# Latent attention in a hybrid decoder layer: a first set of scores for the maxima, a second set laid out as [key, query]

## The chip, the cores and the metric

The kernel runs on one core of a Trainium2 chip. The metric is the device time of one execution in microseconds (us), as the median of the runs shown. A core has five engines that work side by side and wait for each other by semaphores: TensorE (PE; its weight loads are listed apart as PEld), VectorE (DVE), ScalarE (ACT), GpSimd (POOL) and SyncE (SP), which here only issues DMA transfers. Each engine works through its own instructions in a fixed order, so an instruction that waits holds up everything behind it on that engine.

## The reference

Two decoder layers work on one sequence of 1024 tokens of width 1024, in float32. Each layer multiplies x by `w_in`, runs three token mixers on slices of the result, concatenates them, multiplies by `w_o`, normalizes, and ends with a gated feed-forward part. The mixers are stick-breaking attention (4 heads), multi-head latent attention (MLA, 4 heads) and RWKV-7 (8 heads). The change concerns MLA above all, and one instruction of stick-breaking:

```python
def causal_softmax_attention(q, k, v, scale):        # MLA: q, k have 96 columns per head, v has 64
    s = einsum('bhqd,bhkd->bhqk', qb, k) * scale
    s = where(kpos <= qpos, s, neg)
    p = softmax(s, axis=-1)
    return einsum('bhqk,bhkd->bhqd', p, v)

def stick_breaking_attention(q, k, v):               # 4 heads of 64
    z = einsum('bhqd,bhkd->bhqk', qb, k) * scale
    log_keep = where(past, log_sigmoid(-z), 0)
    log_later = cumsum(log_keep, reverse=True) - log_keep
    w = where(past, exp(log_sigmoid(z) + log_later), 0)
    return einsum('bhqk,bhkd->bhqd', w, v)

mix = concatenate([o_sb, o_mla, o_rwkv], axis=-1) @ w_o
x = layer_norm(DEEPNORM_ALPHA * x + mix, ln1_g, ln1_b)
```

## The kernel before

Matmuls that must be exact to float32 are made of three in the format float32r: each operand is split into a high part and a rest, and `mm3` adds high x high, high x rest and rest x high into one accumulator. The values are plain float32.

A layer runs in stages: `phase_a` (projections, MLA's preparation, RWKV), then the attention stage in `run`, then `oproj` (the product with `w_o` and the first normalization), then `ffn`. Every mixer writes its output into `mixd` in DRAM, as 8 blocks of 128 rows (channels) by 1024 tokens; `mix_load(i)` reads all 8 blocks for the 128 tokens of tile i and splits them, and `oproj` takes the tiles from i = 7 down to 0. `wo_load(l, k)` reads row block k of `w_o`; blocks 2 to 5 go into four buffers named `pst`, and blocks 0, 1, 6 and 7 share the two buffers named `raw` with the tiles that `mix_load` reads.

In the attention stage four generators are drawn from in turn, one query block of 128 tokens at a time: two for MLA (`mla`, hp = 0 and 1, each working through two heads) and two for stick-breaking (`stick`). The list `seq`, built from STREAM_ORDER, sets the turns, and MLA_AHEAD blocks of MLA come ahead of them all. The second head of each generator takes its query blocks in falling order (`range(NT)[:: 1 - 2 * pr]`), so that the block of tokens 7 is written early in the second half. A scheduler of the framework then sets the final order on every engine, from the order of the code and the offsets in PRIORITY.

One MLA block (`mla_block`, `mla_post`) works with queries on the partitions: scores [128 queries, up to 1024 keys] in one or two pieces of at most 512 columns (`sc`, two PSUM banks), causal mask by one more matmul, maximum on DVE, the running negative maximum on DVE, exponential on ACT with its row sum, a correction factor and a reciprocal, and the normalization of the probabilities on DVE:

```python
nc.vector.reduce_max(c(0), s, axis=AX.X)
nc.scalar.activation(e[:, a0:a1], s, AF.Exp, scale=sc, bias=c(2), accum_out=c(4))
nc.vector.tensor_scalar(e[:, a0:a1], e[:, a0:a1], st[:, 6:7], None, op0=ALU.mult)
```

`w_transpose` turns the probabilities into [key, query] with one TensorE transpose per 128x128 block and an ACT copy out of PSUM, `attn_out` multiplies them with V, and `av_store` copies 64 rows of the result and issues the store to `mixd`.

One stick-breaking block (`stick_block`, `stick_post`) has two matmuls per piece, a tanh on ACT, a mask on POOL, then on DVE `kp = 0.5 - 0.5 * be` (line 385), a scan and a product; transposes, values and store go as above, through the PSUM banks `pa`.

Of the kernel before, what the change touches and what calls it, by code (L numbers as in the profile page):

```python
# [9 lines left out]
F32 = mybir.dt.float32  # L10
# [31 lines left out]
MLA_AHEAD = 4  # L42
STREAM_ORDER = (-3, 0, 0, 1)
# [26 lines left out]
class Body:  # L70
# [38 lines left out]
    def constants(self):  # L109
# [40 lines left out]
        nc.vector.memset(self.mhalf, -0.5)  # L150
        self.rmse = self.t(cp, [P, 1], "rmse")
# [229 lines left out]
    def stick_post(self, be, kp, i, LL, nb, n, V, hp, pr, wp):  # L381
# [3 lines left out]
        nc.vector.tensor_scalar(kp[:, : LL - 1], be[:, 1:LL], -0.5, 0.5, op0=ALU.mult, op1=ALU.add)  # L385
# [117 lines left out]
    def mla(self, wp, hp):  # L503
        nc = self.nc
        r96 = slice(0, 96)
        for pr in range(2):
            if hp == 0:
                self.mv = self.t(wp, [P, NT, P], "mv")
                nc.sync.dma_start(self.mv, self.mvd[pr])
            V = self.mv  # L510
            rq, rk = (self.t(self.pp_, [P, S], "pst", bufs=4) for _ in range(2))
            nc.sync.dma_start(rq[r96], self.mqd[2 * pr + hp])
            nc.sync.dma_start(rk[r96], self.mkd[2 * pr + hp])
            qh, ql, kh, kl = (self.t(wp, [P, S], f"{n}{hp}", F32R, bufs=1) for n in ("qh", "ql", "kh", "kl"))
            eng = nc.gpsimd if pr else None
            for h, lo, r in ((kh, kl, rk), (qh, ql, rq)):
                nc.scalar.copy(h[r96], r[r96])
                self.lo4(lo, r, h, r96, SPLIT_MLA[pr])
            for i in range(NT)[:: 1 - 2 * pr]:
                self.mla_block(i, pr, hp, (qh[r96], ql[r96], kh[r96], kl[r96]), V, wp)  # L520
                yield

    def mla_block(self, i, pr, hp, qk, V, wp):
        nc = self.nc
        sc = 96 ** -0.5
        qh, ql, kh, kl = qk
        nb, LL = i + 1, (i + 1) * P
        qs = slice(i * P, i * P + P)
        st = self.t(wp, [P, 12], "mst", bufs=4)
        e = self.t(wp, [P, S], "mexp", bufs=3)  # L530
        pcs = self.pieces(LL)
        n = len(pcs)
        for u, (a0, a1) in enumerate(pcs):
            sp = self.pst("sc")
            s = sp[:, : a1 - a0]
            last = u == n - 1
# [3 lines left out]
            c = lambda o, u=u: st[:, o + u : o + u + 1]  # L540
            nc.vector.reduce_max(c(0), s, axis=AX.X)
            if u:
                nc.vector.tensor_scalar(c(2), c(0), -sc, st[:, 2:3], op0=ALU.mult, op1=ALU.min)
            else:
                nc.vector.tensor_scalar(c(2), c(0), -sc, None, op0=ALU.mult)
# [683 lines left out]
```

## Time and profile before

| | us |
|---|---|
| median of 3 runs (lowest, highest) | 3157.64 (3152.78, 3160.75) |
| the profiled execution's own time | 3154.05 |
| span in its profile | 3152.3 |
| attention stage, layer 0: from the first MLA score to the last attention matmul | about 549 to 747 |
| the same, layer 1 | about 2097 to 2306 |

The span begins with the first instruction and ends with the last. A stage is found by the times of its own instructions; the two attention stages together take 407 us, 13% of the span, and the rest is projections, RWKV and the feed-forward part. In the views an engine is busy while one of its instructions runs; matmuls overlap in the array, so that TensorE can be busy nearly all the time and still not issue at its full rate. The time between the starts of neighbouring matmuls tells what one costs when nothing holds it up.

### The profile page before, as it was taken

The numbers are of one execution on the slowest core, as the hardware profiler recorded it, in microseconds if no ns is written. First come the engines' busy times: TensorE is split into PE (matmuls) and PEld (weight loads), VectorE is DVE, ScalarE is ACT, GpSimd is POOL, SyncE is SP. The second block draws the span as 40 slices with busy tenths as digits, with TensorE's granted clock in tenths as the row PEclk, the third lists the DMA queues.
The fourth block names the chain that finished last, engine by engine and source line by source line (L and its number), as shares of the span: only waits on it lengthen the run. The fifth ranks groups of instructions, "written<-read, shape, count | busy, mean of one in ns | idle before, by whom it ended". The sixth has DMA issues, their size and how long they took to land. (4 is left out here: it accounts for less than half of the span.)

```text
span 3152.3 us, 42021 instructions
## 1 busy us (share of the span) xinstructions
PE 2993.2 (95%) x16572; PEld 2421.2 (77%) x16572; DVE 1796.4 (57%) x2842; ACT 1058.6 (34%) x1865; POOL 330.7 (10%) x346
## 2 busy tenths in 40 slices
PE   8998999988999999999999989999789999999998
PEld 6677777776888888888877767777678888888887
DVE  4587764876644444444746877567865444344436
ACT  5444343764122112222144443446532211122220
POOL 0112131132000000000001111311310000000000
PEclk9999899999999999999999999999899999999999
DMA  4344566323421111111234456662235111111111
GB/s 129 97 141 110 169 186 191 97 62 121 149 85 50 51 41 47 54 50 51 64 84 127 108 132 193 178 190 53 81 121 172 54 47 40 43 56 49 54 47 54
DMA packets 339284, 301.79 MB, mean 96 GB/s; under 512 B 25224, under 2 KB 304016, under 8 KB 339088
## 3 DMA queue, kind: packets, MB, share of 16 engines
q1 hardware_dynamic: 339088, 299.11, 32.1%
q8 instruction: 131, 2.15, 0.3%
q14 instruction: 65, 0.53, 0.1%
HBM read 208.87 MB, written 90.18 MB: 95 GB/s over the span
## 5 line engine op out<-in xcount | busy, mean ns | idle before, releaser
L202 PE MATMUL psmm<-xTh,whi 128*128 128x512 f32 x2144 | 852.9, 398 | 0.0
L204 PE MATMUL psmm<-xTh,wlo 128*128 128x512 f32 x2144 | 852.1, 397 | 0.0
L203 PE MATMUL psmm<-xTl,whi 128*128 128x512 f32 x2144 | 852.1, 397 | 0.0
L197 ACT CAST whi<-raw 128x1024 fp32r<-128x1024 f32 x152 | 159.9, 1052 | 1111.3 <-PE psmm L203 1076.1
L204 PEld LDWEIGHTS psmm<-xTh,wlo 128*128 128x128 f32 x2144 | 405.2, 189 | 93.2 <-issue 4.3
L202 PEld LDWEIGHTS psmm<-xTh,whi 128*128 128x128 f32 x2144 | 405.4, 189 | 92.9 <-issue 4.4
L203 PEld LDWEIGHTS psmm<-xTl,whi 128*128 128x128 f32 x2144 | 405.3, 189 | 92.8 <-issue 3.9
L198 DVE TENSOR_TENSOR wlo<-raw,whi 128x1024 fp32r<-128x1024 f32 x122 | 148.8, 1220 | 424.5 <-ACT whi L197 424.5
L1031 DVE TENSOR_TENSOR y<-y,psps 128x512 f32<-128x512 f32 x288 | 196.2, 686 | 171.8 <-PE psps L204 171.4
L202 PE MATMUL psps<-wdh,hh 128*128 128x512 f32 x672 | 266.8, 397 | 0.0
L203 PE MATMUL psps<-wdl,hh 128*128 128x512 f32 x672 | 263.1, 391 | 0.0
L204 PE MATMUL psps<-wdh,hl 128*128 128x512 f32 x672 | 260.1, 391 | 0.0
L894 POOL TENSOR_TENSOR lrs<-lrs,mhalf 128x1 f32<-128x1 f32 x32 | 29.1, 910 | 1637.7 <-DVE lrs L893 1637.7
L202 PEld LDWEIGHTS psps<-wdh,hh 128*128 128x128 f32 x672 | 126.1, 188 | 36.4 <-ACT hh L197 5.5
L204 PEld LDWEIGHTS psps<-wdh,hl 128*128 128x128 f32 x672 | 126.2, 188 | 27.0
L203 PEld LDWEIGHTS psps<-wdl,hh 128*128 128x128 f32 x672 | 126.3, 188 | 25.8
L1006 DVE TENSOR_TENSOR cv<-cv,psmm 128x1024 f32<-128x1024 f32 x44 | 53.7, 1221 | 143.3 <-PE psmm L204 138.4
L198 DVE TENSOR_TENSOR wdl<-raw,wdh 128x1024 fp32r<-128x1024 f32 x42 | 51.4, 1225 | 88.5 <-ACT wdh L197 88.5
L198 POOL TENSOR_TENSOR wlo<-raw,whi 128x1024 fp32r<-128x1024 f32 x30 | 76.0, 2532 | 242.5 <-ACT whi L197 242.4
L312 PE MATMUL pspa<-Aa,mv 128*128 128x128 f32 x576 | 86.4, 298 | 4.4 <-ACT Aa L328 3.8
L312 PEld LDWEIGHTS pspa<-Aa,mv 128*128 128x128 f32 x576 | 77.1, 207 | 17.5 <-ACT Aa L328 15.8
L820 PE MATMUL pspa<-RBl,PSl 128*128 128x128 f32 x512 | 73.4, 292 | 17.2 <-ACT QC L823 11.8
(443 smaller groups left out, 4777.4 us busy)
## 6 DMA issues: line engine op xcount, KB each, us to landing
raw<-in_ffn_w_up_dram SPq DMA_DIRECT2D x88, 512.0 KB
raw<-in_w_in_dram SPq DMA_DIRECT2D x44, 512.0 KB
raw<-in_ffn_w_down_dram SPq DMA_DIRECT2D x44, 512.0 KB
rbd<-RB SPq DMA_DIRECT2D x64, 256.0 KB
PSl<-psd SPq DMA_DIRECT2D x32, 512.0 KB
RBl<-rbd SPq DMA_DIRECT2D x32, 512.0 KB
psd<-Vz SPq DMA_DIRECT2D x64, 128.0 KB
xxd<-X SPq DMA_DIRECT2D x64, 128.0 KB
```

Of the source, the lines that this page charges most:

```text
L197: self.nc.scalar.copy(hi, src)
L198: (eng or self.nc.vector).tensor_tensor(lo, src, hi.bitcast(F32), op=ALU.subtract)
L202: mm(out, lh, rh, start=start, stop=False)
L203: mm(out, lh, rl, start=False, stop=False)
L204: mm(out, ll, rh, start=False, stop=stop)
L312: self.nc.tensor.matmul(av, V[:, j, :], wt[:, j, :], start=j == 0, stop=j == nb - 1)
L820: nc.tensor.matmul(pQ[:, f, e, :], PSh[:, f, h, e, :], RBh[:, f, h, e, :], start=True, stop=True)
L894: nc.gpsimd.tensor_tensor(rs, rs, self.mhalf[:, 0:1], op=ALU.pow)
L1006: nc.vector.tensor_tensor(cv, cv, pg, op=ALU.mult)
L1031: nc.vector.tensor_tensor(y[:, i, hs], y[:, i, hs], ps, op=ALU.add)
```

## The change

MLA becomes one generator that works through the four heads. For head n it computes all scores as before, but only to take the row maxima (`mla_max`). When all 8 query blocks are done, `mla_row` makes a row of the negative maxima: a reduction over the pieces, a split into a float32r part and its rest, one matmul with the identity that turns columns into rows, a copy on ACT, and two DMA transfers inside SBUF that lay the two parts into rows 96 and 97 of the query operand `qh`. The key operand `kh` holds ones in these rows, and the two rests hold zeros, so the second set of scores (`mla_values`), computed as [key, query] for 512 queries at a time, comes with the maximum already taken off. Its exponential on ACT is the moving operand of the product with V directly. Beside the 64 columns of V stand 64 columns of ones, so that the other half of the accumulator holds the row sums; a reciprocal and a product on DVE finish 512 queries, and one store writes them. The values of head n are drawn from beside the maxima of head n + 1, three units for every two query blocks.

Gone are the running maximum, the row sums from ACT, the correction, the normalization on DVE, the transposes of MLA with their copies, and the order of falling query blocks for MLA. The PSUM banks change from two for `sc` and two for `av` to three and one. In stick-breaking, `kp` is now computed on ACT.

```diff
-MLA_AHEAD = 4
-STREAM_ORDER = (-3, 0, 0, 1)
+MLA_AHEAD = 8
...
-        nc.vector.tensor_scalar(kp[:, : LL - 1], be[:, 1:LL], -0.5, 0.5, op0=ALU.mult, op1=ALU.add)
+        nc.scalar.activation(kp[:, : LL - 1], be[:, 1:LL], AF.Identity, scale=-0.5, bias=self.half)
...
+    def mla_tiles(self, wp):
+        for hp in range(2):
+            ts = {n: self.t(wp, [P, S], f"{n}{hp}", F32R, bufs=1) for n in ("qh", "ql", "kh", "kl")}
+            nc.scalar.copy(ts["kh"][96:98], self.ones[96:98].to_broadcast([2, S]))
+            for n in ("ql", "kl"):
+                nc.scalar.mul(ts[n][96:98], self.ones[96:98].to_broadcast([2, S]), 0.0)
+            V = self.t(wp, [P, NT, P], f"mv{hp}", bufs=1)
+            nc.gpsimd.memset(V[:, :, 64 - 64 * hp : 128 - 64 * hp], 1.0)
...
+    def mla(self, wp):
+        self.mla_tiles(wp)
+        prev = iter(())
+        for n in range(5):
+            if n < 4:
+                pr, hp = n // 2, n % 2
+                ts, V, M = self.mla_load(pr, hp)
...
+                nxt = self.mla_values(wp, pr, hp, ts, V)
+            for i in range(NT):
+                if n < 4:
+                    self.mla_max(i, ts, st)
+                for _ in range(1 + i % 2):
+                    next(prev, None)
+                yield
+            for _ in prev:
+                pass
+            if n < 4:
+                self.mla_row(st, ts, M, wp)
+                prev = nxt
...
+    def mla_row(self, st, ts, M, wp):
+        nc.vector.reduce_max(m, st, axis=AX.X)
+        nc.vector.tensor_scalar(M[:, 0:NT], m, -1.0, None, op0=ALU.mult)
+        nc.vector.scalar_tensor_tensor(M[:, NT : 2 * NT], m, -1.0, M[:, 0:NT].bitcast(F32), op0=ALU.mult, op1=ALU.subtract)
+        nc.tensor.matmul(ps[:, 0:P], M, self.identr, start=True, stop=True)
+        nc.scalar.copy(r[0 : 2 * NT], ps[0 : 2 * NT, 0:P])
+        for u in range(2):
+            nc.sync.dma_start(ts["qh"][96 + u : 97 + u, :].bitcast(F32), r[u * NT : u * NT + NT, :].bitcast(F32))
+
+    def mla_values(self, wp, pr, hp, ts, V):
+        qh, ql, kh, kl = (ts[n][0:98] for n in ("qh", "ql", "kh", "kl"))
...
+        for Q in range(2):
+            q0 = Q * 512
+            av = self.pst("av")
+            nj = 4 * Q + 4
+            for j in range(nj):
+                c0 = max(0, j * P - q0)
...
+                self.mm3(s, kh[:, js], kl[:, js], qh[:, cs], ql[:, cs], True, not dg)
+                if dg:
+                    nc.tensor.matmul(s[:, 0:P], self.negm, self.identr, start=False, stop=True)
+                w = self.t(wp, [P, 512], "mexp", bufs=6)
+                nc.scalar.activation(w[:, c0:512], s, AF.Exp, scale=sc)
+                nc.tensor.matmul(av[:, c0:512], V[:, j, :], w[:, c0:512], start=j == 0, stop=j == nj - 1)
+                if j < nj - 1:
+                    yield
+            nc.vector.reciprocal(rs[hr], av[sr])
+            nc.vector.tensor_tensor(ot[hr], av[hr], rs[hr], op=ALU.mult)
+            nc.sync.dma_start(self.mixd[2 + pr][hr, q0 : q0 + 512], ot[hr])
+            yield
...
-                self.psum(c, sc=(512, 2), av=(512, 2))
+                self.psum(c, sc=(512, 3), av=(512, 1))
...
-                for _, _, g in seq:
-                    next(g, None)
+                for t in range(17):
+                    for g in (ms, st[0], ms, st[1]):
+                        next(g, None)
+                for _ in ms:
+                    pass
```

The program built from each kernel shows the order that the scheduler made of it. First TensorE in the middle of layer 0's attention stage. Before, one query block of an MLA head stands as three score matmuls per piece (`pssc`), the mask (L539), then transposes (L327) and values (L312) of earlier blocks:

```order
L202 MATMUL pssc_5107<-kh_831_4959,qh_829_4957 128x512
L203 MATMUL pssc_5107<-kl_832_4960,qh_829_4957 128x512
L204 MATMUL pssc_5107<-kh_831_4959,ql_830_4958 128x512
L312 MATMUL psav_5049<-Aa_4944,mv_4951 128x128 x4
L202 MATMUL pssc_5114<-kh_831_4959,qh_829_4957 128x256
L203 MATMUL pssc_5114<-kl_832_4960,qh_829_4957 128x256
L204 MATMUL pssc_5114<-kh_831_4959,ql_830_4958 128x256
L539 MATMUL pssc_5114<-negm_67,identr_65 128x128
```

Now a unit of the second set (`psav_5232` takes its exponentials; keys and queries have changed sides) stands beside the first set of the next head:

```order
L203 MATMUL pssc_5327<-qh_827_4953,kh_829_4955 128x512
L204 MATMUL pssc_5327<-ql_828_4954,kh_829_4955 128x512
L205 MATMUL pssc_5327<-qh_827_4953,kl_830_4956 128x512
L602 MATMUL psav_5232<-mexp_5324,mv_831_4960 128x512
L313 MATMUL pspa_5302<-Aa_4946,mv_5098 128x128 x3
L599 MATMUL pssc_5327<-identr_65,negm_67 128x128
L203 MATMUL pssc_5358<-kh_835_4966,qh_833_4964 128x512
L204 MATMUL pssc_5358<-kl_836_4967,qh_833_4964 128x512
L205 MATMUL pssc_5358<-kh_835_4966,ql_834_4965 128x512
```

So the products with V come as single matmuls of up to 512 columns, and no transpose of MLA stands between; the one transposing operation left in the stage is that of stick-breaking.

Second, SP's queue around the end of layer 0's attention stage. Before, the load of the first tile for `oproj` (`raw_7063`, tokens 896 to 1023) and the four blocks of `w_o` that go through `raw` stand among the attention stores (`avo`), with some 15 stores still behind them:

```order
L400 DMA mixd_111<-avo_6537 64x128
L912 DMA raw_7063<-mixd_111 128x8x128
L400 DMA mixd_111<-avo_6572 64x128
L972 DMA raw_7069<-in_w_o_dram 128x1024
L400 DMA mixd_111<-avo_6614 64x128
L972 DMA raw_7071<-in_w_o_dram 128x1024
L400 DMA mixd_111<-avo_6651 64x128
L972 DMA raw_7115<-in_w_o_dram 128x1024
L400 DMA mixd_111<-avo_6684 64x128
L400 DMA mixd_111<-avo_6724 64x128
L972 DMA raw_7119<-in_w_o_dram 128x1024
```

Now they stand behind the last stores of the stage (`mot_6729` is MLA's last 512 tokens), with the normalization's parameters and the residual's tiles among them:

```order
L609 DMA mixd_113<-mot_6729 64x512
L401 DMA mixd_113<-avo_6748 64x128
L958 DMA raw_6751<-mixd_113 128x8x128
L1018 DMA raw_6757<-in_w_o_dram 128x1024
L950 DMA gb_6791<-in_ln_g_dram 128x1024
L950 DMA bb_6793<-in_ln_b_dram 128x1024
L1018 DMA raw_6759<-in_w_o_dram 128x1024
L1018 DMA raw_6803<-in_w_o_dram 128x1024
L984 DMA z_6819<-in_x_dram 128x1024
L984 DMA z_6891<-in_x_dram 128x1024
L1018 DMA raw_6807<-in_w_o_dram 128x1024
L958 DMA raw_6872<-mixd_113 128x8x128
```

All five loads that share the two `raw` buffers, and the next tile's load behind them, have moved past the end of the stage.

Third, TensorE at the same place after the change. `psmm_6821` is tile 7 of `oproj`, `psmm_6893` tile 6:

```order
L602 MATMUL psav_6582<-mexp_6724,mv_837_4971 128x128
L328 MATMUL pspa_6743<-ident_60,mexp_6732 128x128
L313 MATMUL pspa_6746<-Aa_4946,mv_5976 128x128
L203 MATMUL psmm_6821<-w0h_5057,whi_6752 128x512
L204 MATMUL psmm_6821<-w0l_5058,whi_6752 128x512
...
L205 MATMUL psmm_6821<-woh_6789,wlo_6753 128x512
L203 MATMUL psmm_6893<-w0h_5057,whi_6873 128x512
L204 MATMUL psmm_6893<-w0l_5058,whi_6873 128x512
L205 MATMUL psmm_6893<-w0h_5057,wlo_6874 128x512
L203 MATMUL psmm_6893<-w0h_5057,whi_6873 128x512
L204 MATMUL psmm_6893<-w0l_5058,whi_6873 128x512
L203 MATMUL psmm_6821<-w0h_5057,whi_6752 128x512
```

The first product of `oproj` needs tile 7 and block 0 of `w_o`, and the second half of tile 7 stands behind five products that need tile 6; nothing of the attention stage stands beside them.

## Rows read from the trace of the kernel before

**Rows 1.** The page, part 1: busy us, share of the span, instructions of each engine.
```profile
PE 2993.2 (95%) x16572; PEld 2421.2 (77%) x16572; DVE 1796.4 (57%) x2842; ACT 1058.6 (34%) x1865; POOL 330.7 (10%) x346
```

**Rows 2.** Busy by stretch: us, PE, PEld, DVE, ACT, POOL; clock, DMA share, GB/s.
```profile
549.00:747.00 198.00, 173.78 (x1213) 149.15 (x1213) 156.88 (x317) 131.07 (x352) 44.89 (x56) 0.96 0.29 78
2097.00:2306.00 209.00, 176.97 (x1252) 152.36 (x1252) 162.46 (x328) 135.03 (x360) 47.82 (x58) 0.96 0.28 78
590.00:650.00 60.00, 57.38 (x416) 49.59 (x415) 46.02 (x102) 40.21 (x116) 6.14 (x16) 1.00 0.11 27
2305.00:2325.00 20.00, 14.42 (x50) 10.19 (x49) 11.60 (x9) 8.16 (x9) 5.19 (x2) 0.83 0.70 213
```

**Rows 3.** Waits of PE: layer 0's stage (first row), layer 1's (second); total, times, longest.
```profile
PE pspa L327 <- DVE mexp L388: 9.8, 9, 3.1
...
PE pspq L376 <- POOL qh L361: 7.5, 1, 7.5
```

**Rows 4.** Timeline of PE, layer 0: start, us, operation, how many.
```profile
640.45 0.29 PE L202 MATMUL pssc<-kh,qh 96*128 96x256 f32 x1
640.58 0.28 PE L203 MATMUL pssc<-kl,qh 96*128 96x256 f32 x1
641.78 0.93 PE L327 MATMUL psav<-ident,mexp 128*128 128x128 f32 x7
666.49 2.05 PE L312 MATMUL psav<-Aa,mv 128*128 128x128 f32 x16
745.35 0.49 PE L312 MATMUL pspa<-Aa,mv 128*128 128x128 f32 x2
760.09 0.39 PE L202 MATMUL psmm<-woh,whi 128*128 128x512 f32 x1
760.32 0.39 PE L203 MATMUL psmm<-wol,whi 128*128 128x512 f32 x1
763.34 0.39 PE L204 MATMUL psmm<-woh,wlo 128*128 128x512 f32 x1
```

**Rows 5.** Groups of DVE, layer 0's stage: busy us, mean ns, idle before and releaser.
```profile
L541 DVE TENSOR_REDUCE mst<-pssc 128x1 f32<-128x512 f32 (+3 forms) x48 | 26.1, 548 | 7.6 <-PE pssc L204 5.4 <-PE pssc L539 2.1
L561 DVE TENSOR_SCALAR mexp<-mexp,mst 128x256 f32<-128x256 f32 (+3 forms) x32 | 12.3, 388 | 0.2
L559 DVE TENSOR_SCALAR mexp<-mexp,mst 128x512 f32<-128x512 f32 (+1 forms) x16 | 8.6, 535 | 0.5
L385 DVE TENSOR_SCALAR pd<-mexp 128x255 f32<-128x255 f32 (+5 forms) x11 | 5.5, 498 | 3.2 <-POOL mexp L384 3.2
L545 DVE TENSOR_SCALAR mst<-mst 128x1 f32<-128x1 f32 x32 | 4.5, 141 | 0.1
L555 DVE SCALAR_TENSOR_TENSOR mst<-mst 128x1 f32<-128x1 f32 x16 | 4.2, 266 | 11.9 <-ACT mst L554 11.9
L552 DVE RECIPROCAL mst<-mst 128x1 f32<-128x1 f32 x16 | 2.4, 153 | 4.2 <-ACT mexp L546 4.2
```

**Rows 6.** Groups of ACT, the same stretch.
```profile
L328 ACT COPY Aa<-psav 128x512 f32<-128x512 f32 (+3 forms) x48 | 21.7, 479 | 3.7 <-PE psav L327 3.2
L546 ACT ACTIVATION_READ_ACCUMULATOR mexp<-pssc,mst 128x1 f32 x48 | 9.5, 197 | 0.0
L399 ACT ACTIVATE avo<-psav 64x128 f32<-64x128 f32 x32 | 8.7, 270 | 11.1 <-PE psav L312 5.2 <-ACT Aa L328 1.9 <-ACT mst L554 1.5
```

**Rows 7.** Timelines of SP, ACT and DVE, layer 0's handover to `oproj`; last, POOL's group.
```profile
701.13 0.38 SPq L912 DMA_DIRECT2D raw<-mixd  x1
...
755.23 0.38 SPq L912 DMA_DIRECT2D raw<-mixd  x1
...
759.35 1.05 ACT L197 CAST whi<-raw 128x1024 fp32r<-128x1024 f32 x1 [7.40 <-DMA raw<-mixd]
...
760.43 1.23 DVE L198 TENSOR_TENSOR wlo<-raw,whi 128x1024 fp32r<-128x1024 f32 x1 [1.86 <-ACT whi L197]
...
L198 POOL TENSOR_TENSOR w0l<-raw,w0h 128x1024 fp32r<-128x1024 f32 x2 | 6.0, 2978 | 8.1 <-ACT w0h L197 8.1
```

More of the change, by code (lines that the diff above doesn't have):

```diff
@@ L150, in constants @@
         nc.vector.memset(self.mhalf, -0.5)
+        self.half = self.t(cp, [P, 1], "half")
+        nc.vector.memset(self.half, 0.5)
         self.rmse = self.t(cp, [P, 1], "rmse")
@@ L504, in mla, with mla_load @@
+    def mla_load(self, pr, hp):
         nc = self.nc
         r96 = slice(0, 96)
[L506 to L521, printed above, removed]
@@ L523, in mla_block @@
-    def mla_block(self, i, pr, hp, qk, V, wp):
+        ts, V, M = self.mx[hp]
+        rq, rk = (self.t(self.pp_, [P, S], "pst", bufs=4) for _ in range(2))
+        nc.sync.dma_start(rq[r96], self.mqd[2 * pr + hp])
+        nc.sync.dma_start(rk[r96], self.mkd[2 * pr + hp])
+        nc.sync.dma_start(V[:, :, 64 * hp : 64 * hp + 64], self.mvd[pr][:, :, 64 * hp : 64 * hp + 64])
+        for h, lo, r in (("kh", "kl", rk), ("qh", "ql", rq)):
+            nc.scalar.copy(ts[h][r96], r[r96])
+            self.lo4(ts[lo], r, ts[h], r96, SPLIT_MLA[pr])
@@ L524, in mla_block, with mla_max @@
+        return ts, V, M
+    def mla_max(self, i, ts, st):
         nc = self.nc
-        sc = 96 ** -0.5
-        qh, ql, kh, kl = qk
-        nb, LL = i + 1, (i + 1) * P
+        qh, ql, kh, kl = (ts[n][0:96] for n in ("qh", "ql", "kh", "kl"))
+        LL = (i + 1) * P
         qs = slice(i * P, i * P + P)
-        st = self.t(wp, [P, 12], "mst", bufs=4)
-        e = self.t(wp, [P, S], "mexp", bufs=3)
         pcs = self.pieces(LL)
-        n = len(pcs)
         for u, (a0, a1) in enumerate(pcs):
@@ L535, in mla_block @@
             s = sp[:, : a1 - a0]
-            last = u == n - 1
+            last = u == len(pcs) - 1
             self.mm3(s, qh[:, qs], ql[:, qs], kh[:, a0:a1], kl[:, a0:a1], True, not last)
@@ L539, in mla_block @@
                 nc.tensor.matmul(sp[:, a1 - a0 - P : a1 - a0], self.identr, self.negm, start=False, stop=True)
[L540 to L545, printed above, removed]
-            nc.scalar.activation(e[:, a0:a1], s, AF.Exp, scale=sc, bias=c(2), accum_out=c(4))
@@ L547, in mla_block @@
[L547 to L564 removed]
+            nc.vector.reduce_max(st[:, i, u : u + 1], s, axis=AX.X)
@@ L1162, in run @@
             with ExitStack() as c:
-                self.psum(c, sc=(512, 2), av=(512, 2))
+                self.psum(c, sc=(512, 3), av=(512, 1))
                 aw = self.pool(c, "attn", bufs=2, side=side)
-                ms = [self.mla(aw, hp) for hp in range(2)]
+                ms = self.mla(aw)
                 self.wt4 = self.t(self.ip, [P, 6, NT, P], "Aa")
@@ L1170, in run @@
                 for _ in range(MLA_AHEAD):
-                    next(ms[0])
+                    next(ms)
                 cc.close()
@@ L1176, in run @@
                 st = [self.stick(aw3, self.ip, hp) for hp in range(2)]
-                seq = sorted([(t + o, n, g) for n, (g, o) in enumerate(zip((ms[0], st[0], ms[1], st[1]), STREAM_ORDER)) for t in range(17)], key=lambda x: x[:2])
-                for _, _, g in seq:
-                    next(g, None)
+                for t in range(17):
[3 more added lines that the diff above has]
+                    pass
                 nxt = self.mix_load(NT - 1)
```

37 lines of the change are left out of this document (20 added, 17 removed).

## The prediction

> **What bounds the kernel now.** I read the page's first part, then busy time by stretch, then the waits, then timelines. TensorE is busy 2993 of the span's 3152 us [rows 1], so time can be won or lost only where TensorE waits or gets other work. Outside the two attention stages and the steps behind them the edit touches nothing, so the stages are the place: 198 and 209 us, 407 together [rows 2]. There the reader is to see three things: TensorE is busy only 88% and 85% of the time; VectorE is next with 157 of 198 and 162 of 209 us (79% and 78%); ScalarE has 131 of 198. In the best minute of the stage, 590 to 650, TensorE is busy 57.4 of 60 us. What it waits for elsewhere is partly VectorE (9.8 us in layer 0 behind stick-breaking's product, line 388), partly GpSimd (7.5 us in layer 1 behind the split of queries, line 361) [rows 3]. The bound is thus TensorE's own work with a steady loss through its suppliers.
>
> Because overlapped matmuls all count as busy, I count work by spacing instead. At full speed 512 columns cost 0.23 us (760.09 to 760.32), 256 about 0.13 (640.45 to 640.58); 384 lie between, 0.18; a transpose costs (0.93 - 0.27)/6 = 0.11; one record of a 128-column product with V, two of which make a block, (2.05 - 0.27)/15 = 0.119 [rows 4].
>
> **TensorE's work per layer, before.** One head's scores are 12 pieces: five of 512, three of 384, three of 256 and one of 128 columns, 2.17 us, times three matmuls and four heads = 26, plus 32 masks of a block's cost, 3: 29. The transposes are 4 x 36 = 144 at 0.11 = 16; the products 288 at 0.119 = 34. Stick-breaking has two matmuls per piece (17), and the same transposes and products (50): 67. Together 146 to 147. That is 147/198 = 0.74 of layer 0's stage and 147/209 = 0.70 of layer 1's, 0.72 on the whole. In the best minute 416 records at the stage's mean of 147/1213 = 0.121 us make 50.4, or 0.84 of 60 us [rows 2].
>
> **After.** The second scores hold the same 4608 columns a head, with their masks: +29. Gone are MLA's transposes: -16. The products with V move the same columns in fewer records: 0 to -3, taken -2. The four row matmuls are nothing. So 158, 11 more per layer.
>
> **VectorE per layer.** Lines 559, 561, 545, 555 and 552 go: 8.6 + 12.3 + 4.5 + 4.2 + 2.4 = 32; line 385 goes to ScalarE, 32 times about 0.5 = 16 [rows 5]. Line 555's 11.9 us behind ScalarE goes too. The maxima stay (26.1). New are eight products of about 0.65 and four row steps of 0.55: 7. New too are eight reciprocals of 64 x 512 out of PSUM, the change's unknown price. Below, such a tile in one pass costs what line 541's pass does, 0.55 us; above, the one-element reciprocal takes 153 ns against 141 for a plain step of that size, and 12 ns for each element makes 6.3, with the pass about 6.8. One row of one element can't tell a fixed cost from one per element; I take 3.3, half. VectorE then has 157 - 48 + 7 + 26 = 142 (120 to 170 at the ends).
>
> **ScalarE.** MLA's copies (21.7), sum reads (9.5) and output copies (8.7) go [rows 6]; 32 keeps of about 0.6 come (19), four row copies and six fillings of 1024 columns, 1.05 at most each (line 197's cast [rows 7]): 131 falls to about 118. It is no bound before or after, and I price it at nothing; if VectorE were no longer the slower supplier, it would be ScalarE's exponentials that are late next, since the same set of exponentials stays.
>
> **The row's chain.** At each of four head ends the negative maxima pass VectorE, TensorE, ScalarE and two DMAs inside SBUF, before the second scores can start. Stick-breaking and, for three heads, the next head's maxima cover it. A load takes 4.1 us from issue to use [rows 7], so with some 3 for the engines one uncovered end costs about 7; I price none, keeping 14 for the two last ends in the range.
>
> **The stage.** Its time is work over rate. Upwards the rate is bounded by the best minute, 0.84 (188 us a stage, -31 for both); downwards by 0.72 to 0.74 with VectorE no better off (427 for both, +20). I take 0.80, two thirds of the way up: a tenth of VectorE's load and a chain through ScalarE for every block go, but GpSimd's wait and stick-breaking's chain stay. Twice 158/0.80 = 395, -12.
>
> **The handover.** Before, tile 7's load was issued at 701.13, 45 us ahead of the last attention product (745.35 + 0.49 = 745.84, call it T0); tile 7's last product starts at 763.34, T0 + 17.5 [rows 4, 7]. The delay came from blocks of `w_o` that take turns in the two `raw` buffers. In the new order the tile's load and all four blocks stand behind the last stores, which need MLA's last 512 tokens. So: reciprocal and product 4.0, the store's issue 0.4 and its landing about 2.5 (no row shows it; under the 4.1 of a larger load), then the load of tile 7, 4.1 (755.23 to 759.35), and its split, 1.05 on ScalarE and 1.23 on VectorE [rows 7]: T0 + 13. On SP block 0 of `w_o` waits behind that load, lands at T0 + 11.5 and is split at 15.5 (1.05 and GpSimd's 2.98); block 1 follows in the tile's buffer (13 to 20), block 6 in block 0's (15.5 to 23.5), block 7 behind block 1, and tile 6 in block 6's buffer, landing at 27.7 and split at 30. The five products of tile 6 that stand ahead of tile 7's second half hold it until then; 24 products of 0.23 end the tile, T0 + 35.5. That is 18 later; less 1 for the five products already done, and 1 more because ten transfers of 512 KB at the 213 GB/s of layer 1's handover [rows 2] take 24.6 of these 30 us and meet. **+18 per layer, +36 for both.** Ends: +9 (one-pass reciprocal, loads of 3 us that don't meet) and +24 (the slow reciprocal, loads queued behind each other). No work covers it: nothing else is on TensorE's list there. The clock of layer 1's handover is 0.83 against 0.96 in the stage [rows 2], so an idle TensorE also loses some speed afterwards; that is inside the upper end.
>
> **Sum.** Against the profiled execution's 3154 us: -12 + 36 = +24, **3178**. The median of the runs shown, 3157.6, is 3.6 higher, well within the 0.3% (9.5 us) that a measurement of this kernel can tell. This case's own range: rate 0.78 to 0.83 (-2 to -26) and handover +13 to +22 each give 3154 to 3196.
>
> **Rivals.** *Faster: the stage's suppliers were the whole loss.* The rate goes beyond the best minute, to 0.88 (359 us, -48), the reciprocal is one pass, and the handover +13 or 14 each: -21, **3133**. It decides from a rate of about 0.85, where -35 pays the forecast's +36. For it: VectorE's 79% and the waits of [rows 3]; wide products instead of 128-column ones. Against it: no minute of the old stage shows more than 0.84. The Trainium skill, "Perfetto Trace Analysis", section "Identifying the Most-Contended Engine", judges TensorE by weight loads rather than by matmul busy time and would have the engine of highest occupancy improved first. By that rule the stage's bound is VectorE (79% against 149 of 198, 75%, of weight loads), which this change relieves, and the result is this rival; the rows bear it out as far as the two numbers go. Chance 0.20.
>
> *Cancels.* Rate 0.84 to 0.85 and a handover of +16 each: -33 + 32, about **3153**, within 0.3%. Chance 0.15.
>
> *Slower still: the reciprocal.* At 6.8 us, eight of them (54) undo VectorE's relief (170 against 157); each also stops the one bank `av`, so the next unit's product waits behind it, and each layer's last one stands open in the handover. Rate 0.75: 421, +14; handover +19 to 20 with the overlap of loads kept, +38: **3206**. It decides from about 5 us a piece, where VectorE is back at 157. The Trainium skill, "VectorE: DVE Perf Modes", section "First, the fixed hardware budget", says that the reciprocal is an iterative divide with a repeat count of 8. An estimate by that page, eight passes of 512 at one element per 0.96 GHz cycle, would be 4.3 us: VectorE 150, at a rate of 0.79 400 us (-7), the handover +19 each, the sum 3185; no row here shows it. Chance 0.23.
>
> **Numbers.** Forecast 0.42, the rest as above. Nearly all of the forecast's cases and all of the third rival's are slower by over 0.3%: 0.65; within 0.3% 0.15; faster 0.20. The range reaches half into the faster rival at 3136 and past the slow one to 3222, and leaves out about 2 in 10.
>
> **What would show it.** In the profile after: the reciprocal's mean (3 us; 0.6 or 7 are the rivals'); the stage from the first MLA score to the last product, near 197 us; VectorE's busy time there, near 142; the load of tile 7 issued some 7 us after the last product, and tile 7's last product near T0 + 35. A stage under 187 us, or a handover under 25 us, proves the forecast wrong on the fast side; waits of TensorE for the bank `av` or for the row's DMA proves it wrong on the slow one.

## The result, and the profile after

The changed kernel takes 3250.44 us (median of four runs, 3246.35 to 3254.85), the kernel before 3155.89 in the same comparison. The ratio is 1.0298 with a 95% interval of 1.0279 to 1.0318: slower by 3%, some 95 us, where 20 to 24 were forecast. The profiled execution took 3254.85, its span is 3253.1.

The page's first part of the changed kernel (busy us, share of the span, instructions), against [rows 1]:

```profile
PE 3048.8 (94%) x16260; PEld 2429.6 (75%) x16260; DVE 1781.1 (55%) x2547; ACT 1051.2 (32%) x1665; POOL 334.3 (10%) x358
```

VectorE and ScalarE have less to do, as meant, and TensorE 56 us more. Where the time went is seen by stretches. I cut both traces at the same events: a stage from the first MLA score (in layer 1 from RWKV's last product, which comes just before it) to the last product with V; the handover from there to the first transposition of `oproj`'s result.

| profiled execution, us | before | after | difference |
|---|---|---|---|
| stage, layer 0 | 196.6 | 232.3 | +35.7 |
| stage, layer 1 | 202.8 | 231.8 | +29.0 |
| handover, layer 0 | 23.5 | 39.1 | +15.6 |
| handover, layer 1 | 24.4 | 39.4 | +15.0 |
| layer 1's projections and RWKV | 514.1 | 522.5 | +8.4 |
| all else | 2190.9 | 2188.0 | -2.9 |

The handovers came near the forecast (+18 each). The stages, forecast 12 us shorter together, are 65 longer. The 8.4 us in layer 1's RWKV belong to no instruction of the change: the same stretch took between 511 and 522 us in the profiles of the other runs below, and it was long where its mean granted clock was low (0.95 at 522.5 us, 0.97 at 514.1, 0.98 at 511.0), so I count it as variation of single executions.

Busy time by stretch after (length; PE, PEld, DVE, ACT, POOL with their counts; granted clock, DMA share, GB/s): both stages, four pieces of layer 0's, its handover. It answers to [rows 2].

```profile
547.80:780.60 232.80, 192.97 (x1053) 149.19 (x1052) 145.34 (x171) 116.17 (x241) 43.74 (x57) 0.90 0.21 54
2159.50:2391.70 232.20, 192.69 (x1054) 149.31 (x1052) 146.13 (x170) 116.46 (x242) 42.73 (x57) 0.90 0.21 54
...
564.00:572.00 8.00, 2.05 (x7) 1.85 (x8) 3.73 (x8) 3.62 (x5) 0.36 (x2) 0.58 0.57 168
572.00:580.00 8.00, 7.82 (x27) 5.74 (x26) 3.68 (x6) 3.90 (x8) 0.29 (x1) 0.57 0.95 256
580.00:590.00 10.00, 9.18 (x49) 7.00 (x48) 7.51 (x10) 5.83 (x15) 1.17 (x4) 1.00 0.10 23
676.00:684.00 8.00, 3.73 (x11) 2.42 (x11) 5.63 (x4) 2.98 (x5) 7.93 (x7) 0.62 0.42 131
781.00:814.00 33.00, 17.14 (x53) 11.82 (x54) 15.15 (x8) 10.14 (x10) 10.59 (x4) 0.65 0.61 208
```

The two stages before, cut at the same events as here:

```profile
549.00:746.00 197.00, 173.72 (x1213) 149.15 (x1213) 156.88 (x317) 130.10 (x351) 44.89 (x56) 0.96 0.29 78
2102.00:2305.00 203.00, 172.69 (x1220) 149.00 (x1218) 159.20 (x319) 130.73 (x351) 46.08 (x56) 0.96 0.28 76
```

VectorE's 145 us against 142 forecast and ScalarE's 116 against 118: their part of the sum held. TensorE is idle 40 us of each stage where it was idle 23 and 30, and busy 19 and 20 us longer, of which the prediction's count of work explains 11. Its mean clock in the stage is 0.90 where it was 0.96: at two levels, 1.2 and 2.4 GHz, that is about 45 us of layer 0's stage at the lower one, where it was about 17. The other 8 or 9 us of the longer busy time I put down to this clock; that is an estimate from these rows, and no run holds the clock still.

In two of the pieces TensorE does little: it is busy 2.05 us from 564 to 572 and 3.73 from 676 to 684. Behind the first, 572 to 580 is full of matmuls at a clock of 0.57. What it waited for (layer 0's stage; total us, times, longest; [rows 3] before):

```profile
PE pspa L328 <- DVE mexp L389: 17.7, 13, 4.9
PE pspq L377 <- POOL qh L362: 6.2, 1, 6.2
PE pspq L377 <- DVE qh L362: 4.5, 1, 4.5
PE pssc L575 <- DVE mm L573: 2.6, 1, 2.6
```

The last three rows are new in layer 0 at this length (GpSimd's split cost 0.6 us there before). Two are starts of stick-breaking heads (line 377), which now fall on the ends of MLA heads (line 575), so that nothing ahead of them on TensorE's list fills the wait. In layer 1 the wait for GpSimd is not new: it was 7.5 us before [rows 3] and is 6.2 now. The first row is stick-breaking's own chain, 9.8 us before [rows 3]. TensorE's timeline after, at these places and at the end (start, us, operation, idle before and releaser):

```profile
565.40 0.45 PE L575 MATMUL pssc<-identr,mm 128*128 128x128 f32 x1 [2.63 <-DVE mm L573]
...
571.25 0.45 PE L377 MATMUL pspq<-kh,qh 128*128 128x128 f32 x1 [4.55 <-DVE qh L362]
...
572.02 0.63 PE L204 MATMUL pssc<-ql,kh 98*128 98x512 f32 x1
572.45 0.63 PE L205 MATMUL pssc<-qh,kl 98*128 98x512 f32 x1
...
679.04 0.80 PE L377 MATMUL pspq<-kh,qh 128*128 128x512 f32 x1 [6.15 <-POOL qh L362]
...
778.92 0.47 PE L328 MATMUL pspa<-ident,mexp 128*128 128x128 f32 x1 [4.94 <-DVE mexp L389]
779.75 0.80 PE L313 MATMUL pspa<-Aa,mv 128*128 128x128 f32 x2 [0.35 <-ACT Aa L329]
787.94 0.79 PE L203 MATMUL psmm<-w0h,whi 128*128 128x512 f32 x1 [7.39 <-ACT w0h L198]
791.09 0.79 PE L204 MATMUL psmm<-w0l,whi 128*128 128x512 f32 x1 [2.36 <-POOL w0l L199]
...
813.80 0.39 PE L205 MATMUL psmm<-woh,wlo 128*128 128x512 f32 x1
```

After the first hole 512 columns cost 0.43 us (572.02 to 572.45) instead of 0.23: the lower of the two levels, 1.2 GHz. The last product with V ends at 780.55; tile 7's last product of its own starts at 813.80, 33.3 later (35.5 forecast, 17.5 before). VectorE's groups (layer 0's stage), which answer to [rows 5]:

```profile
L606 DVE RECIPROCAL mrs<-psav 64x512 f32<-64x512 f32 x8 | 26.8, 3355 | 9.2 <-PE psav L602 9.1
L566 DVE TENSOR_REDUCE mst<-pssc 128x1 f32<-128x512 f32 (+3 forms) x48 | 25.6, 551 | 36.4 <-PE pssc L205 24.5 <-PE pssc L565 11.6
L388 DVE TENSOR_TENSOR_SCAN LA<-LA,ones 128x255 f32<-128x255 f32 (+4 forms) x10 | 14.2, 1417 | 14.1 <-ACT LA L386 14.1
...
L608 DVE TENSOR_TENSOR mot<-psav,mrs 64x512 f32<-64x512 f32 x8 | 5.5, 687 | 0.2
```

The reciprocal takes 3.36 us (3.3 was taken). VectorE now waits for scores (36.4 us in front of line 566, where the same pass waited 7.6 before [rows 5]). And at the stage's end, VectorE's timeline shows what a long instruction does to those behind it:

```profile
774.02 3.35 DVE L606 RECIPROCAL mrs<-psav 64x512 f32<-64x512 f32 x1 [2.54 <-PE psav L602]
777.40 0.42 DVE L388 TENSOR_TENSOR_SCAN pd<-pd,ones 128x127 f32<-128x127 f32 x1
777.85 0.69 DVE L608 TENSOR_TENSOR mot<-psav,mrs 64x512 f32<-64x512 f32 x1
778.58 0.29 DVE L389 SCALAR_TENSOR_TENSOR mexp<-mexp,pd 128x128 f32<-128x128 f32 x1
```

Stick-breaking's last scan needs 0.42 us and stands behind the reciprocal, and TensorE waits 4.94 for what follows it. SP's timeline closes the chain: MLA's store, stick-breaking's last store, then tile 7's load and `w_o`.

```profile
778.57 0.45 SPq L609 DMA_DIRECT2D mixd<-mot  x1
780.88 0.45 SPq L401 DMA_DIRECT2D mixd<-avo  x1
781.42 0.54 SPq L958 DMA_DIRECT2D raw<-mixd  x1
782.01 0.57 SPq L1018 DMA_DIRECT2D raw<-in_w_o_dram  x1
```

Tile 7's load is issued 0.9 us after the last product, where the prediction looked for 7: MLA's reciprocal, product and store were done before that product ended. Two signs that it gave for the slow side did not come: TensorE waits 0.2 us for the bank `av` in layer 0's stage, and 0.4 us for the row's DMA in layer 1's.

### The profile page after: what moved, and what is told of

Read it like the earlier page. It is cut to its first block, busy times and chain, and to the rows that moved or that the text cites. A ratio compares the mean times of both kernels' runs of the same rounds, so it can differ in the third digit from the quotient of the medians.

```text
span 3253.1 us, 40843 instructions
## 1 busy us (share of the span) xinstructions
PE 3048.8 (94%) x16260; PEld 2429.6 (75%) x16260; DVE 1781.1 (55%) x2547; ACT 1051.2 (32%) x1665; POOL 334.3 (10%) x358
## 4 chain that ended last, share of the span: by engine, by line
PE 74%; DVE 10%; issue 9%; DMA 3%; ACT 2%; POOL 1%; SPq 0%; POOLq 0%; DVEq 0%; ACTq 0%
PE psmm L205 15%; PE psmm L203 15%; PE psmm L204 15%; PE psps L203 5%; PE psps L204 5%; PE psps L205 5%; PE pspa L866 2%; DVE pd L751 1%; PE pspi L810 1%; PE pspa L313 1%; DVE LA L747 1%; PE psmt L214 1%; PE pspa L708 1%; PE psav L602 1%; DMA LA<-xxd 1%
## 5 line engine op out<-in xcount | busy, mean ns | idle before, releaser
L204 PEld LDWEIGHTS psps<-wdl,hh 128*128 128x128 f32 x672 | 126.2, 188 | 25.7
L328 PE MATMUL pspa<-ident,mexp 128*128 128x128 f32 x288 | 61.7, 304 | 34.8 <-DVE mexp L389 34.8
```

The source lines that it names most:

```text
L204: mm(out, lh, rl, start=False, stop=False)
L328: nc.tensor.transpose(pt[:, j * P : j * P + P], w[:, (j0 + j) * P : (j0 + j + 1) * P], self.ident)
```

## The experiments

Times are medians against 3250.4 (changed) or 3155 (before, 3151.6 to 3155.9 from one comparison to the next). The changed kernel was timed in the first comparison only, so a difference of 4 us or less to 3250.4 tells nothing. In the tables "stage" and "handover" are cut as above, layer 0 / layer 1.

**First round: order or suppliers.** The first theories were O, that the stages lost their time by the new order of turns, and S, that the slower supplier (VectorE or ScalarE) still sets the pace.

e1 puts one line back:

```diff
-        nc.scalar.activation(kp[:, : LL - 1], be[:, 1:LL], AF.Identity, scale=-0.5, bias=self.half)
+        nc.vector.tensor_scalar(kp[:, : LL - 1], be[:, 1:LL], -0.5, 0.5, op0=ALU.mult, op1=ALU.add)
```

> The changed kernel with one line of stick-breaking put back: keep is computed on VectorE again. Theory O (order: the 64 us that the two stages lost come from where the new list of turns puts MLA against stick-breaking, so that TensorE has nothing else at the starts of stick-breaking's heads and at the end): within 8 us of the changed kernel's 3250. Theory S (suppliers: ScalarE now stands twice in stick-breaking's chain, and VectorE's 32 us a layer behind ScalarE's keep hold TensorE up): 20 to 40 us faster, 3210 to 3230.

e2 takes out the reciprocal's length:

```diff
-            nc.vector.reciprocal(rs[hr], av[sr])
+            nc.vector.tensor_copy(rs[hr], av[sr])
```

> The changed kernel with MLA's reciprocal replaced by a plain copy of the same 64 x 512 out of PSUM, so the division by the row sums is left out; sixteen reciprocals of 3.36 us become sixteen passes of about 0.7, 21 us of VectorE a layer. Theory O: only the piece at each stage's end and one long stall near 611 us go, 5 to 15 us, 3235 to 3245. Theory S with VectorE as the slower supplier: most of the 42 us of VectorE comes back, 3208 to 3220.

e3 changes one number:

```diff
-MLA_AHEAD = 8
+MLA_AHEAD = 16
```

> The changed kernel with MLA_AHEAD 16 instead of 8: two heads' steps of MLA stand ahead of stick-breaking, MLA's last stores and with them tile 7's load come before stick-breaking's last blocks, and oproj's first products stand beside these. Nothing is computed differently. Theory O: the handover falls by 12 to 14 us a layer, the last 5 us wait and the hole at 564 to 572 with its half clock go as well, 40 to 70 us in all, 3180 to 3210. Theory S: the handover alone, about 25 us, and the stages stay 232 us long: 3225.

e4 moves two blocks of `w_o`:

```diff
                 for t in range(17):
...
+                    if t == 12:
+                        wr = [self.wo_load(l, k) for k in range(2)]
+                        for k in range(2):
+                            self.split(self.w0h[:, k], self.w0l[:, k], wr[k], nc.gpsimd)
...
-                wr = [self.wo_load(l, k) for k in range(6)]
+                wr += [self.wo_load(l, k) for k in range(2, 6)]
```

> The changed kernel with blocks 0 and 1 of w_o loaded and split four rounds before the end of the stage, while the two raw buffers are free; tile 7's load keeps its place behind the last stores. It prices the chain of raw buffers in the handover alone: 8 us a layer by the chain of the prediction (the two blocks' transfers and splits leave it, tile 7's transfer and split stay), 16 us in all, 3234; if tile 7's transfer is what all waits for, under 5 us, 3245 to 3250.

| | median us | stage | handover |
|---|---|---|---|
| e1 keep on VectorE | 3244.66 | 229.9 / 231.0 | 38.9 / 39.8 |
| e2 copy for reciprocal | 3231.66 | 224.0 / 223.2 | 40.0 / 39.0 |
| e3 MLA_AHEAD 16 | 3232.31 | 246.9 / 246.0 | 22.5 / 22.5 |
| e4 `w_o` early | 3238.51 | 233.4 / 232.1 | 28.7 / 29.7 |

Both theories fall in this form. Keep's place is worth 1 to 2 us a layer (the rest of e1's 6 lies, in the profiles, in RWKV's stretch, 515.2 against 522.5). The reciprocals cost 8.3 and 8.6 us a layer of the 21 of VectorE's time that the copy saves: more than O said, far from all. In e2 VectorE's row and TensorE's first wait (layer 0's stage) read

```profile
L606 DVE COPY mrs<-psav 64x512 f32<-64x512 f32 x8 | 5.5, 688 | 11.7 <-PE psav L602 11.6
...
PE pspa L328 <- DVE mexp L389: 12.3, 14, 2.3
```

So 5.4 of the 8.3 us of layer 0 come out of TensorE's wait for stick-breaking's product (17.7 in the changed kernel): the reciprocal stood in front of that chain on VectorE's list.

e3 took the handover back entirely, and the stage lost 14 of these 17 us a layer again: layer 0's stage and handover together went from 271.4 to 269.4. That its median is 18 lower lies, in the profiles, in layer 1's RWKV (511.0 against 522.5) and in products of `oproj` already done by then (3 a layer). MLA heads and stick-breaking heads still end in the same turn, and TensorE (layer 0) now stands before stick-breaking's second head longer than before:

```profile
704.22 0.39 PE L378 MATMUL pspy<-kl,qh 128*128 128x512 f32 x1
716.28 0.80 PE L377 MATMUL pspq<-kh,qh 128*128 128x512 f32 x1 [11.67 <-POOL qh L362]
```

e4 shortens the handover by 10.4 and 9.7 where 8 were expected (its median is 12 lower, where 16 were): the two `raw` buffers' turns are most of the 15 that the handover grew.

**Second round: work or chains.** Theory W now says that what TensorE does more is simply added; C that coinciding heads and stick-breaking's chain make the loss. e5 and e6 change a number each:

```diff
-MLA_AHEAD = 8
+MLA_AHEAD = 12
```

> The changed kernel with MLA_AHEAD 12. With 8 or 16 an MLA head ends in the same turn in which a stick-breaking head ends or begins, so both reload at once (the holes at 564 and 673 us); with 12 they are half a head apart. Theory C (coinciding heads and stick-breaking's chain make the holes): 30 to 45 us faster than the changed kernel's 3250, 3205 to 3220, and more than MLA_AHEAD 16 gave. Theory W (the stage grew because TensorE's work grew and what isn't overlapped adds to it): what MLA_AHEAD 16 gave, 15 to 20, 3230 to 3235.

```diff
-SPLIT_STICK = (0, 4)
+SPLIT_STICK = (0, 0)
```

> The changed kernel with the low parts of the second stick-breaking heads computed on VectorE (1.2 us a tile) instead of GpSimd (four pieces of 1.4 us a tile). Theory C: TensorE's 6.2 us wait for GpSimd at 673 to 679 and the half clock after it shrink by half, 3 to 6 us a layer, 3238 to 3244. Theory W: no difference, 3245 to 3252.

e7 (changed kernel) and e8 (kernel before):

```diff
-                self.mm3(s, kh[:, js], kl[:, js], qh[:, cs], ql[:, cs], True, not dg)
+                nc.tensor.matmul(s, kh[:, js], qh[:, cs], start=True, stop=not dg)
```

> The changed kernel with only the first of the three float32r matmuls in the second set of scores, so that set is not exact to float32; the other engines do what they did. It takes 2 x 9 = 18 us of TensorE's work out of each layer's stage, more than the 11 by which the change raised it. Theory W: at least 36 us in all, 3214 or less. Theory C: the waits stay, half or less, 3232 to 3240.

```diff
+            self.mm3(s, qh[:, qs], ql[:, qs], kh[:, a0:a1], kl[:, a0:a1], True, True)
             self.mm3(s, qh[:, qs], ql[:, qs], kh[:, a0:a1], kl[:, a0:a1], True, not last)
```

> The kernel before with each MLA score piece computed twice into the same bank (the first result is overwritten), so TensorE has 26 us more work a layer and every other engine and the order stay the same. It prices work alone in the old order. Theory W: 52 us or more, 3205 to 3225 against 3154. Theory C: TensorE fills its waits with it, 20 to 30 us, 3175 to 3185.

| | median us | stage | handover |
|---|---|---|---|
| e5 MLA_AHEAD 12 | 3223.93 | 235.3 / 227.4 | 29.0 / 28.1 |
| e6 split on VectorE | 3233.81 | 225.2 / 225.2 | 39.2 / 39.9 |
| e7 18 us less work | 3210.88 | 212.5 / 211.5 | 39.2 / 38.8 |
| e8 26 us more work (before) | 3195.16 | 222.3 / 219.9 | 27.3 / 23.8 |

e7's stages are 19.8 and 20.3 us shorter for 18 us of work; e8's are 25.7 and 17.1 longer for 26. That is 1.1 us of stage for each us of work in e7, 1.0 and 0.7 in e8, whose median (44 us more) lies between the two expectations. VectorE's load is about the same with and without the extra work (busy by stretch, the stage of layer 0, e8; VectorE is the third busy time, 156.88 before):

```profile
545.00:768.00 223.00, 196.37 (x1363) 166.79 (x1360) 158.48 (x319) 132.84 (x352) 45.06 (x56) 0.99 0.25 69
```

C holds beside it in part. The split on VectorE gives 7 us a layer, more than the 3 to 6 expected; how much of that the kernel before would gain from it too was not tried. e5 gains 26 us in all, between the two expectations, but not where C looked for it: its handovers are 10.1 and 11.3 shorter, its two stages together 1.4. There TensorE no longer waits for GpSimd, and its wait for line 389 falls from 17.7 to 6.9 us; but the hole in front of the first stick-breaking head is still 5.2 us, waits for ScalarE grow from 5 to 17, and the clock of layer 0's stage is 0.86.

**Third round: the removed parts by themselves, and the sum.** e9 and e10 start from the kernel before:

```diff
-        wt = self.w_transpose(self.wt4[:, self.sn % 6], e, nb)
+        wt = e[:, : nb * P].rearrange("p (a b) -> p a b", b=P)
```

> The kernel before without MLA's transposes and their copies: the probabilities go to the product with V as they lie, so MLA's output is not the reference's. It removes by itself what the change removed on TensorE, 144 x 0.11 = 16 us a layer, and 22 us of ScalarE's copies. Theory W (TensorE's work adds one to one, so the removed work must come back in full): 30 to 40 us faster than before, 3112 to 3122. Rival R (transposes stood in TensorE's gaps, so that removing them gave little while the added scores cost all): 5 to 20 us, 3132 to 3147.

```diff
-        if n == 1:
-            nc.vector.reciprocal(st[:, 6:7], st[:, 4:5])
-        else:
...
-                nc.vector.tensor_scalar(e[:, a0:a1], e[:, a0:a1], st[:, 6:7], None, op0=ALU.mult)
```

> The kernel before with MLA's correction, reciprocal and normalization left out (lines 552 to 561), so its output is not divided by the row sums; about 27 us of VectorE a layer and the hop through ScalarE go, TensorE's work stays. It removes by itself what the change removed on VectorE. The prediction's rate of 0.80 asks this to be worth at least 13 us a layer: 3125 or less. Theory W: under 5 us a layer, 3144 to 3154.

e11 is e1's line the other way round, in the kernel before; e12 is the changed kernel with e1, e4, e5 and e6 together.

> The kernel before with stick-breaking's keep on ScalarE, the change's smallest part alone: 16 us a layer from VectorE, 19 us to ScalarE. Theory W: within 6 us of before, as it was within 6 us of the changed kernel when put back there. Theory S (VectorE is the slower supplier): 10 to 20 us faster, 3132 to 3142.

> The changed kernel with MLA_AHEAD 12, blocks 0 and 1 of w_o loaded early, the splits on VectorE and keep on VectorE: everything of order and placing that helped, the same work on TensorE and the same reciprocals. If the parts add (26, 6 more a layer of handover beside MLA_AHEAD 12, 13 and 4): about 3190 to 3200, and what is left against before, 35 to 45, is the work (11 a layer) and the reciprocals (8 a layer), theory W. If order was all: 3155 to 3170.

| | median us | stage | handover |
|---|---|---|---|
| e9 no transposes (before) | 3123.51 | 184.4 / 186.7 | 24.2 / 24.2 |
| e10 no normalization (before) | 3155.04 | 200.6 / 201.8 | 25.0 / 25.1 |
| e11 keep on ScalarE (before) | 3154.51 | 199.3 / 198.7 | 25.2 / 24.9 |
| e12 combined | 3207.10 | 224.4 / 226.5 | 20.9 / 23.6 |

This round decides. The transposes' 16 us a layer come back as 12 and 16 (ratio 0.9911, 0.9894 to 0.9927), just short of what W expected. MLA's copies leave with them (ScalarE is busy 113 us of the stage instead of 130), so e9 does not price TensorE's work alone. The normalization, which is more of VectorE's time than the whole change took away, comes back as nothing: ratio 1.0001, 0.9991 to 1.0010. Its stage (layer 0, busy by stretch) has VectorE at 136 us instead of 157, and is no shorter (200.6 and 201.8 against 196.6 and 202.8):

```profile
548.00:749.00 201.00, 172.54 (x1220) 149.13 (x1215) 135.91 (x223) 127.58 (x335) 45.47 (x56) 0.96 0.29 77
```

TensorE's waits there show why: those for VectorE's line 388 fell from 9.8 to 4.1, and others came up in their place. By what ended them, the waits for VectorE fell from 15 to 9 us, those for ScalarE rose from 5 to 12 and those for GpSimd from 2 to 6.

```profile
PE pspq L376 <- POOL qh L361: 6.3, 1, 6.3
PE psav L327 <- ACT mexp L546: 5.2, 7, 2.2
PE pspa L327 <- DVE mexp L388: 4.1, 4, 1.8
```

Keep moved to ScalarE in the kernel before also gives nothing (1.0001, 0.9992 to 1.0011); but it puts 22 us onto ScalarE (152 busy against 130), so it prices the swap and not the relief alone. e12 stays 52 us above before, and 7 to 17 above what was expected: e5 and e6 mend the same wait for GpSimd (layer 1's stage is 227.4 with e5 alone and 226.5 here). In the profiles its handovers are 34 us shorter than the changed kernel's, its stages 13.

**Fourth round: what is left.** e13 is e12 with one matmul in the first set of scores, e14 also has the reciprocal on ScalarE, e15 is e13 with e2's copy.

```diff
-            self.mm3(s, qh[:, qs], ql[:, qs], kh[:, a0:a1], kl[:, a0:a1], True, not last)
+            nc.tensor.matmul(s, qh[:, qs], kh[:, a0:a1], start=True, stop=not last)
```

> e12 with one of the three float32r matmuls in the first set of scores: that set only gives the maxima, and the softmax is the same whatever is taken off alike above and below, so the result stays exact. It takes 2 x 9 = 18 us of TensorE's work out of each layer, which is then below that of before (140 against 147). Theory W: 34 to 38 us faster than e12's 3207, 3169 to 3173, and still slower than before by the reciprocals. Rival (the rest is in the new structure's chains, not in work): under 20 us faster, 3187 or more.

```diff
-            nc.vector.reciprocal(rs[hr], av[sr])
+            nc.scalar.activation(rs[hr], av[sr], AF.Ln)
+            nc.scalar.activation(rs[hr], rs[hr], AF.Exp, scale=-1.0)
```

> e13 with the reciprocal taken from VectorE: ScalarE makes it as exp of minus the logarithm, two passes of 64 x 512 and two more loads of its function tables each (1.3 us by the one in the stage). Theory W with the reciprocals as the rest: 10 to 17 us faster than e13, 3153 to 3162, level with before. If the table loads stand in stick-breaking's chain as the reciprocals did: within 5 us of e13.

> e13 with the reciprocal replaced by a plain copy, so the division by the row sums is left out, as in e2. If the parts add: 15 to 18 us faster than e13's 3179, 3161 to 3164, and 6 to 8 us are left to the new structure's other chains (row of maxima, coinciding reloads). If the reciprocals were all that was left: 3153 to 3158.

| | median us | stage | handover |
|---|---|---|---|
| e13 one matmul for maxima | 3179.05 | 213.5 / 213.9 | 21.0 / 23.5 |
| e14 and reciprocal on ScalarE | 3198.92 | 223.8 / 223.7 | 23.5 / 23.2 |
| e15 e13 with copy | 3157.05 | 201.4 / 202.8 | 20.8 / 22.2 |

e13 gains 28 of the 34 to 38 expected: its stages are 10.9 and 12.6 shorter for 18 us of work, and TensorE's clock in layer 0's stage falls from 0.93 to 0.88. e14 lost 20 instead of gaining: the logarithm and the exponential of one unit make ScalarE load its tables again and again, and these stand in front of what follows on ScalarE's list. TensorE's waits for ScalarE grow from 6 to 18 us in layer 0's stage and from 8 to 20 in layer 1's (ScalarE's groups, layer 0's stage and the start of its handover):

```profile
L606 ACT ACT_TABLE_LOAD x8 | 10.3, 1283 | 0.1
...
L607 ACT ACT_TABLE_LOAD x6 | 7.7, 1283 | 0.1
L607 ACT ACTIVATE mrs<-mrs 64x512 f32<-64x512 f32 x8 | 5.0, 626 | 0.1
L606 ACT ACTIVATE mrs<-psav 64x512 f32<-64x512 f32 x8 | 4.7, 593 | 0.1
```

e15 is level with before (1.0009, 0.9999 to 1.0018). So the reciprocals are worth 22 us in all. 3157 lies in the range that was expected if they were all that was left; but with them and the added work gone the new structure still gains nothing, though it has 7 us less work a layer than before. TensorE's idle time is about what it was (29 and 28 us against 23 and 30), and its clock in the stage is 0.92 and 0.91 against 0.96, so that the 7 us seem to go into the clock rather than into waits. No version of the new structure beats the kernel before; e13 is the quickest that computes the same as the changed kernel.

## Why the prediction was wrong

Point by point, by its own steps:

- **TensorE's work, +11 a layer: held.** e7, e8 and e9 each measured a term (the second set, the first set, the transposes) and found 0.7 to 1.1 us of stage per us of work counted by spacing; e13 found 0.6 and 0.7 for the first set in the changed kernel. e9's price holds ScalarE's copies too.
- **VectorE 142, ScalarE 118, reciprocal 3.3: held** (145, 116, 3.36).
- **The handover, +18 a layer: held in size** (+15.6 and +15.0), and e4 shows two thirds of it to be the turns of the `raw` buffers. The first link was wrong: MLA's reciprocal, product and store, 6.9 us, do not stand behind the last product. The load of tile 7 came 6 us earlier than forecast and tile 7's last product 2.2 earlier, so the steps between took about 4 us longer than priced, and the total agrees partly by luck. No run shows the 2.5 us taken for the store's landing.
- **"I take 0.80, two thirds of the way up": failed.** It is the step that put the result outside the range. Work over stage time came out at 158/232 = 0.68, below the 0.72 to 0.74 that was taken as the lower end. The step rested on the belief that relief of VectorE raises TensorE's rate; e10 gave the kernel before such relief, 21 us of it, and found nothing. VectorE's 79% was busy time, not a bound: TensorE waited for one chain at a time, and another took its place. The lower end was wrong as well, since it was taken from the old order: in the new one TensorE idles 40 us a stage and has a clock of 0.90. A smaller slip is that the 407 us began 5 us ahead of layer 1's stage; cut as here, before is 399, and the forecast's 395 would have been -4.
- **"I price none" of the heads' ends: the row's chain nearly held, what stands beside it was left out.** The row itself costs TensorE 2.6 us once in layer 0. But at 564 and 673 us an MLA head ends where stick-breaking's begins, and stick-breaking's reload costs 4.6 and 6.2 more, with half clock behind the first (0.57 to 580) and 0.62 to 0.74 at the second (676 to 692). The sum has no term for these; e6 is worth 7 a layer at the second place alone.
- **The reciprocal was priced as 26 us of VectorE's time, and as nothing beyond:** taking 21 us of VectorE's time out of the normalization gave 0 (e10, kernel before), out of the reciprocals 8 a layer (e2, changed kernel). That the difference is the 3.36 us for which each one blocks VectorE's list is argued from the timeline at 774 and from the shorter wait in e2; the two kernels differ in more than this.

Of the two stages' +65, single trials on the changed kernel give back 17 with the reciprocals (e2), 14 with the split at the coinciding ends (e6) and 3 with keep (e1); the added work, priced at one to one, makes about 22, 56 in all. These need not add up, as e12's parts did not, and 7 of e6's 14 stand in layer 1, where TensorE waited for the same split before. So 9 to 16 are not settled. The hole at 571, which no run changed by itself, is a candidate, and so are the single generator for MLA and the single bank `av`, which no run took back. What closes is the chain of runs: order, placing and keep (e12) take 43 us off the 3250, one matmul for the maxima (e13) 28, the copy (e15) 22, and that is level with before.

The slow rival named the reciprocal with a rate of 0.75 and 3206. Its reciprocal of 6.8 us, its undoing of VectorE's relief and its wait for the bank `av` did not come (3.36 us, 145 us busy, 0.2 us); that a reciprocal holds up what others wait for, at the stage's end above all, did. The faster rival rested on the Trainium skill, "Perfetto Trace Analysis", section "Identifying the Most-Contended Engine": improve the engine of highest occupancy first. Here this was VectorE by the prediction's reading, and the runs disagree with the rule: e10 lowered VectorE to 136 of 201 us at no gain, while e9, which lowered TensorE's work by 16 us a layer and ScalarE's copies with it, gained 31 in all. The estimate worked out from the Trainium skill for the reciprocal ("VectorE: DVE Perf Modes", section "First, the fixed hardware budget": eight passes, 4.3 us) is above the measured 3.36.

## What to carry to other kernels

Before a busy engine is relieved for the sake of another, try the relief alone: leaving the normalization out takes one small edit and showed that 21 us of VectorE a layer were worth nothing, while the same trial with TensorE's work (do it twice, or leave two of three matmuls away) showed a price of 0.6 to 1.1 us for each us. Where several streams share an engine, look where their reloads fall: a hole here cost its length and then up to 8 us at half clock. (Moving the turns alone, as in e5, shortened the handovers and left the stages as long.) Ask of a long instruction what stands behind it on its engine's list: eight of 3.36 us cost some 8 us a layer here, and the same time in pieces of 0.1 to 0.5 us cost nothing in the kernel before.

## What the runs showed of the hardware

- The reciprocal of 64 x 512 out of PSUM takes 3.36 us against 0.69 for a copy or a product of the same size: 6.6 ns for each element of a row. The one-element rows of before had bounded it by 12.
- ScalarE's change between logarithm and exponential costs 1.28 us each time (14 loads at the two lines, 18 us in a stage of e14); the two functions themselves take 0.6 us each.
- TensorE stood still for 6 of the 8 us from 564 to 572, at a mean granted clock of 0.58; the clock was 0.57 in the next 8, in which it was busy 7.82, and 1.00 from 580 on. The Trainium skill, "TensorE: Matmul & The Clock Gate", section "Part 1: The HAM clock gate (the "warmup" mystery)", says that the slow clock is the default and that activity releases it; the trace agrees.
- In e8, TensorE with 26 us more work had a clock of 0.99 in the stage against 0.96, and in e13, with 18 us less than e12, it was 0.88 against 0.93. So part of the price of work may come from the clock; no run here separates the two.
